# The RWKV state of head 0 copied out of PSUM by ScalarE, that of head 1 by VectorE

## The chip, the cores and the metric

The kernel runs on one core of a Trainium2 chip. The metric is the time of one execution on the device in microseconds (us). The profile comes from one further execution under the hardware profiler; its own time is its span, from the first instruction to the last.

## What is computed

The program is one inference step of a one-layer decoder trunk. A prompt of 1024 tokens with 16 meta tokens ahead of it, and 8 running sequences of 8 new tokens each, go through an input projection, two mixers side by side (RWKV-7 time mixing with 8 heads of 64, and an mLSTM with 4 heads of 128), a gated merge, and an MLP with 4096 hidden columns. What matters here is the RWKV recurrence, which the reference writes token by token:

```
def _rwkv7_step(S, inp):
    r, w, k, v, kk, a = inp
    sa = jnp.einsum('bhvk,bhk->bhv', S, -kk)
    S = S * w[:, :, None, :] + sa[..., None] * (kk * a)[:, :, None, :] + v[..., None] * k[:, :, None, :]
    return S, jnp.einsum('bhvk,bhk->bhv', S, r)
```

Each head has a state S of 64 x 64 that is carried from token to token.

## The kernel before, in words

**Chunks.** The kernel turns the recurrence into chunks of 64 tokens: the work inside a chunk is made into matmuls, and only the state goes from chunk to chunk. The 1152 padded token places make 18 chunks. They are taken in groups of three (`G = 3`), six groups for each of four pairs of heads (`j`), so 24 groups in all. Of the last group of each pair only the first two chunks carry the prompt's state on (its third holds the running sequences), and its second chunk ends in the separate tile `S`, at L889.

**Stages.** Each group passes through four stages, a generator each: `stage_a` (decays and keys, and the strictly triangular matrix X1), `stage_b` (the inverse of a triangular matrix, by forward substitution and three block steps), `stage_c` (the state recurrence and the outputs) and `stage_d` (normalisation of the outputs). The substitution of `stage_b` is a chain of 15 pairs on VectorE, L757 (`tmp`) and L759 (`x`), each of which reads what the one ahead of it wrote. `run_step` runs one step of a software pipeline: stage c of one group beside stage b of the next group and stage a of the one after it, in the hand-written order `ORDER`. Between the pieces, `pull` puts matmuls of the input projection (L277, L279, L281) into TensorE's order as filler.

**The recurrence.** In `stage_c`, for each chunk `c`, two matmuls (one per head, L885) multiply the state tile `Vs` by the transition `GH` into one PSUM tile `pS`: head 0 in partitions 0 to 63, head 1 in partitions 64 to 127. Then two instructions of VectorE (L893, 64 x 65 elements each) scale each half by the decay `lam` and copy it out of PSUM, into the place of `Vs` from which the next chunk's L885 reads. `pS` comes from `cbank()`, a PSUM pool with a single buffer (`c=1`), so the next L885 needs that bank to be read out, too. These copies stand 128 times in the program: 64 chunks of two heads. The output matmuls of a chunk (`ymm`, L841) are issued behind the next chunk's L885.

**What sets the order.** TensorE's order is the program's own order (`manual_schedule` for PE), and so are the fillers' places in it. For VectorE, ScalarE and GpSimd a scheduler at build time decides which instruction stands behind which. It sees an instruction of every stage of the step, and interleaves them. On the chip each engine takes its queue strictly in that order.

Names used below: `wa` (L662, L663 on ScalarE, L669 on VectorE) and `cc` (L672, VectorE) are the decay of stage a; `li`, `lam`, `lx` (L677, L678, L676, ScalarE) come from it; L673, L684, L685, L686, L687 on GpSimd make its keys `KB` and receptances `RB`; L682 and L730 on VectorE are the last of stage a's vector work; L761 and L764 close the substitution.

## Time and profile before

| | us |
|---|---|
| median of 3 runs | 2103.38 |
| lowest, highest | 2100.62, 2105.63 |
| the profiled execution: span | 2102.9 |
| TensorE busy (matmuls) | 1974.6 |
| VectorE busy | 1364.2 |
| ScalarE busy | 704.7 |
| GpSimd busy | 511.1 |

PE is TensorE, PEld its weight loads, DVE is VectorE, ACT is ScalarE, POOL is GpSimd. In a timeline each row gives the start, the duration, the engine, the line and operation, the tiles, and in brackets how long the engine was idle before it and which instruction ended that wait. The RWKV part with its copies lies between about 130 and 850 us of the span.

### The profile page before, as it was taken

Reading aid. Unit: us, or ns where it says so; the run is one execution under the profiler, and the core shown is the slowest. Engines: PE = TensorE matmul, PEld = TensorE weight load, DVE = VectorE, ACT = ScalarE, POOL = GpSimd, SP = SyncE. Lnnn points to the kernel's source line nnn. Section 1 sums busy time; section 2 is a strip of 40 time slices with the busy share of each in tenths; the row PEclk is TensorE's granted clock in tenths of the full one; section 3 lists DMA queues with packets and bytes.
Section 4 is the critical chain, followed back from the end, with each engine's and each line's share of the span. In section 5 each row is a group of like instructions: output and inputs, shape, how many; then the busy total and the mean of one; then the engine's idle time right before and its main releaser. Section 6 shows DMA issues by size and latency. Waiting matters only on the chain.

```text
span 2102.9 us, 32130 instructions
## 1 busy us (share of the span) xinstructions
PE 1974.6 (94%) x12325; PEld 1788.6 (85%) x12325; DVE 1364.2 (65%) x3503; ACT 704.7 (34%) x1654; POOL 511.1 (24%) x392
## 2 busy tenths in 40 slices
PE   8989898999989899989899997999999999999996
PEld 8978788888888788889888886988889999998895
DVE  6478778877887888578776639624444444445447
ACT  7333333333334333254654323331112222222122
POOL 2322122212222222122432404221112212112125
PEclk9999999999999999999999999999999999999998
DMA  5221111212111112231656614211111111111114
GB/s 162 62 68 54 46 52 57 64 45 66 55 51 49 52 61 66 64 107 62 230 175 200 215 60 145 71 51 41 41 41 41 50 51 41 51 41 43 49 32 164
DMA packets 148491, 161.59 MB, mean 77 GB/s; under 512 B 20429, under 2 KB 121607, under 8 KB 148337
## 3 DMA queue, kind: packets, MB, share of 16 engines
q1 hardware_dynamic: 148336, 159.54, 23.7%
q8 instruction: 97, 1.59, 0.3%
q14 instruction: 58, 0.47, 0.1%
HBM read 121.98 MB, written 37.27 MB: 76 GB/s over the span
## 4 chain that ended last, share of the span: by engine, by line
PE 48%; DVE 12%; ACT 2%; DMA 2%; issue 2%; POOL 1%; DVEq 0%; SPq 0%; ACTq 0%; POOLq 0%
PE g L215 11%; PE g L213 11%; PE g L214 11%; PE g L281 2%; PE g L277 2%; PE g L279 2%; PE g L1719 1%; DVE acc L1097 1%; PE g L1619 1%; PE g L1621 1%; PE g L1620 1%; POOL gb L1549 1%; DVE tmp L757 1%; DVE nw L173 1%; DVE ACC L1775 1%
## 5 line engine op out<-in xcount | busy, mean ns | idle before, releaser
L201 POOL TENSOR_TENSOR lo<-raw,hi 128x1024 fp32r<-128x1024 f32 x116 | 280.4, 2422 | 1039.6 <-ACT hi L199 1033.5
L281 PE MATMUL g<-u,lo 128*128 128x414 f32 (+4 forms) x1120 | 388.6, 347 | 1.8 <-POOL lo L201 1.8
L277 PE MATMUL g<-u,hi 128*128 128x414 f32 (+4 forms) x1120 | 387.0, 346 | 2.0 <-ACT gst L527 1.1
L279 PE MATMUL g<-u,hi 128*128 128x414 f32 (+4 forms) x1120 | 386.3, 345 | 0.0
L215 PE MATMUL g<-mg,lo 128*128 128x384 f32 (+1 forms) x768 | 252.3, 328 | 0.0
L213 PE MATMUL g<-mg,hi 128*128 128x384 f32 (+1 forms) x768 | 252.2, 328 | 0.0
L214 PE MATMUL g<-mg,hi 128*128 128x384 f32 (+1 forms) x768 | 252.1, 328 | 0.1
L199 ACT CAST hi<-raw 128x1024 fp32r<-128x1024 f32 x124 | 128.6, 1048 | 342.5 <-PE g L1719 250.9
L1755 DVE TENSOR_TENSOR ACC<-g,ACC 128x512 f32<-128x512 f32 x234 | 159.0, 689 | 111.2 <-PE g L215 105.1
L277 PEld LDWEIGHTS g<-u,hi 128*128 128x128 f32 x1120 | 219.4, 196 | 7.9 <-issue 1.5
L281 PEld LDWEIGHTS g<-u,lo 128*128 128x128 f32 x1120 | 219.6, 196 | 7.4 <-POOL lo L201 2.2
L279 PEld LDWEIGHTS g<-u,hi 128*128 128x128 f32 x1120 | 219.2, 196 | 4.3 <-issue 0.2
L213 PE MATMUL g<-hi,ah 128*128 128x512 f32 (+1 forms) x515 | 202.9, 394 | 0.0
L214 PE MATMUL g<-lo,ah 128*128 128x512 f32 (+1 forms) x515 | 202.7, 394 | 0.0
L215 PE MATMUL g<-hi,ah 128*128 128x512 f32 (+1 forms) x515 | 202.4, 393 | 0.0
L214 PEld LDWEIGHTS g<-mg,hi 128*128 128x128 f32 x768 | 144.6, 188 | 1.1 <-DVE mg L1594 0.4
L213 PEld LDWEIGHTS g<-mg,hi 128*128 128x128 f32 x768 | 144.7, 188 | 0.6
L215 PEld LDWEIGHTS g<-mg,lo 128*128 128x128 f32 x768 | 144.7, 188 | 0.0
L215 PEld LDWEIGHTS g<-hi,ah 128*128 128x128 f32 x515 | 96.7, 188 | 23.0
L213 PEld LDWEIGHTS g<-hi,ah 128*128 128x128 f32 x515 | 96.6, 188 | 22.3
L214 PEld LDWEIGHTS g<-lo,ah 128*128 128x128 f32 x515 | 96.7, 188 | 22.0
L757 DVE TENSOR_TENSOR tmp<-NR,x 128x45 f32<-128x45 f32 (+4 forms) x360 | 97.5, 271 | 20.8 <-DMA NR<-ndr 13.2
(852 smaller groups left out, 3609.3 us busy)
## 6 DMA issues: line engine op xcount, KB each, us to landing
raw<-in_w_in_dram SPq DMA_DIRECT2D x44, 512.0 KB
raw<-in_w_ff_up_dram SPq DMA_DIRECT2D x32, 512.0 KB
raw<-in_w_ff_down_dram SPq DMA_DIRECT2D x32, 512.0 KB
NR<-ndr SPq DMA_DIRECT2D x24, 384.0 KB
gscr<-gst SPq DMA_DIRECT2D x16, 544.0 KB
xt<-in_x_prompt_dram SPq DMA_DIRECT2D x15, 512.0 KB
ga<-gscr SPq DMA_DIRECT2D x8, 544.0 KB
pscr<-ga SPq DMA_DIRECT2D x8, 544.0 KB
```

The costliest lines, as they stand in the source:

```text
L173: V.scalar_tensor_tensor(out=o, in0=a, scalar=c, in1=b, op0=f, op1=g)
L199: nc.scalar.copy(out=hi, in_=raw)
L201: (eng or PO).tensor_tensor(out=lo, in0=raw, in1=hi.bitcast(F32), op=ALU.subtract)
L213: mm(ps, lhsT=wh, rhs=xh, start=(i == 0), stop=False)
L214: mm(ps, lhsT=wh, rhs=xl, start=False, stop=False)
L215: mm(ps, lhsT=wl, rhs=xh, start=False, stop=(i == last))
L277: mm(ps, lhsT=hi[:, k], rhs=xh, start=(k == 0), stop=False)
L279: mm(ps, lhsT=hi[:, k], rhs=xl, start=False, stop=False)
L281: mm(ps, lhsT=lo[:, k], rhs=xh, start=False, stop=(k == 7))
L757: V.tensor_tensor(out=tmp[:, :, :n], in0=NR[:, s + 1:16, :, s].rearrange("p t c -> p c t"), in1=x[:, :, s:s + 1].broadcast_to([128, G, n]) ...
L1097: V.scalar_tensor_tensor(out=acc[:, a:a + m], in0=R[:, a + t_:a + t_ + m], scalar=cw(t_), in1=acc[:, a:a + m], op0=ALU.mult, op1=ALU.add)
L1755: V.tensor_tensor(out=ACC[:, i, cs], in0=ps, in1=ACC[:, i, cs], op=ALU.add)
```

## The change

For each chunk, head 0's copy becomes an activation (function Copy, with the decay as its scale) on ScalarE, and head 1's stays on VectorE:

```
-                    for h, s in enumerate(HP):
-                        V.tensor_scalar(out=Vn[s, cn, h], in0=pS[s], scalar1=lc[s], scalar2=None, op0=ALU.mult)
+                    act(out=Vn[HP[0], cn, 0], in_=pS[HP[0]], func=AF.Copy, scale=lc[HP[0]])
+                    V.tensor_scalar(out=Vn[HP[1], cn, 1], in0=pS[HP[1]], scalar1=lc[HP[1]], scalar2=None, op0=ALU.mult)
```

In the changed kernel L892 is ScalarE's copy of head 0 and L893 VectorE's copy of head 1. The order of TensorE's instructions and of the DMAs is the same in both. On the other three engines the scheduler places instructions anew, around the copies above all. Three places:

**VectorE, the first chunk's copies in the step whose copies run at 357 us.** `x 128x3x9` is a row of the substitution chain with nine columns left; the engines whose signals an instruction waits for stand in brackets. Before:

```order
L759 TENSOR_TENSOR x<-x,tmp 128x3x9 [waits DVE_49]
L893 TENSOR_SCALAR Vs<-c,lam 64x65 [waits PE_49]
L893 TENSOR_SCALAR Vs<-c,lam 64x65
L757 TENSOR_TENSOR tmp<-NR,x 128x3x8 [waits DVE_49]
L669 TENSOR_SCALAR wa<-wa 128x384 [waits Activation_49]
L759 TENSOR_TENSOR x<-x,tmp 128x3x8 [waits DVE_49]
L672 SCALAR_TENSOR_TENSOR cc<-Ct,wa 128x192 [waits DVE_49]
L757 TENSOR_TENSOR tmp<-NR,x 128x3x7 [waits DVE_49]
```

The same place in the changed kernel:

```order
L759 TENSOR_TENSOR x<-x,tmp 128x3x9 [waits DVE_49]
L757 TENSOR_TENSOR tmp<-NR,x 128x3x8 [waits DVE_49]
L759 TENSOR_TENSOR x<-x,tmp 128x3x8 [waits DVE_49]
L757 TENSOR_TENSOR tmp<-NR,x 128x3x7 [waits DVE_49]
L669 TENSOR_SCALAR wa<-wa 128x384 [waits Activation_49]
L893 TENSOR_SCALAR Vs<-c,lam 64x65 [waits Activation_49]
L759 TENSOR_TENSOR x<-x,tmp 128x3x7 [waits DVE_49]
L672 SCALAR_TENSOR_TENSOR cc<-Ct,wa 128x192 [waits DVE_49]
```

Head 0's copy is gone, and head 1's now stands behind four instructions (L757, L759, L757, L669) that stood behind it before. It no longer waits for TensorE but for ScalarE, that is for head 0's copy.

**ScalarE in the same step.** Before:

```order
L663 ACTIVATE wa<-a,PRH 128x192
L677 ACTIVATE li<-cc 128x192 [waits DVE_49]
L678 ACTIVATE lam<-cc 128x192
L676 ACTIVATE lx<-wa 128x192 [waits Pool_49]
L689 COPY bdb<-KB 64x3x64 [waits DVE_49]
```

In the changed kernel:

```order
L663 ACTIVATE wa<-a,PRH 128x192
L892 ACTIVATE Vs<-c,lam 64x65 [waits PE_49]
L677 ACTIVATE li<-cc 128x192 [waits DVE_49]
L678 ACTIVATE lam<-cc 128x192
L676 ACTIVATE lx<-wa 128x192 [waits Pool_49]
L892 ACTIVATE Vs<-c,lam 64x65 [waits PE_49]
L689 COPY bdb<-KB 64x3x64 [waits DVE_49]
```

The first chunk's copy stands right behind L663, the second chunk's right behind `lx`.

**GpSimd, stage a in the step at 217 us** (stage a of the last group of the first pair of heads). Before:

```order
L684 TENSOR_SCALAR wa<-wa,PRM,OKA 128x192
L685 TENSOR_TENSOR wa<-wa,Zk 128x192
L686 TENSOR_TENSOR KB<-wa,li 128x3x64
L687 TENSOR_TENSOR RB_735<-Zr,lam 128x3x64
L854 TENSOR_TENSOR smpD<-Ct,lam 128x256
```

In the changed kernel:

```order
L684 TENSOR_SCALAR wa<-wa,PRM,OKA 128x192
L687 TENSOR_TENSOR RB_735<-Zr,lam 128x3x64
L685 TENSOR_TENSOR wa<-wa,Zk 128x192
L854 TENSOR_TENSOR smpD<-Ct,lam 128x256
L686 TENSOR_TENSOR KB<-wa,li 128x3x64
```

The keys `KB` (L686), for which VectorE's L730 waits, moved behind L687 and L854.

## The prediction

> **What bounds the kernel now.** I read the page's busy times first, then the busy times of the RWKV part alone, then what TensorE waits for there.

> ```profile
> PE 1974.6 (94%) x12325; PEld 1788.6 (85%) x12325; DVE 1364.2 (65%) x3503; ACT 704.7 (34%) x1654; POOL 511.1 (24%) x392
> 120.00:870.00 750.00, 683.31 (x5300) 621.03 (x5300) 594.17 (x2036) 262.05 (x722) 166.33 (x190) 0.95 0.19 56
> ```

> TensorE is the engine that sets the end. In the 750 us around the recurrence it is idle for 750.0 - 683.3 = 66.7 us, VectorE is busy for 79%, ScalarE for 35%. The waits of TensorE in that stretch (us in total, times, the longest):

> ```profile
> PE c L885 <- DVE Vs L893: 47.0, 27, 2.6
> PE a L697 <- POOL KB L686: 5.5, 3, 1.9
> ```

> So 47.0 of the 66.7 us are one wait: the matmul of the next chunk (L885) waits for the copies that the change touches, 27 times. The timeline of one step shows which of its chunks. Its three L885 groups (four rows each, two heads in two passes), with the wait ahead in brackets:

> ```profile
> 353.23 0.39 PE L885 MATMUL c<-Vs,GH 128*64 128x65 f32 x4
> 358.03 0.49 PE L885 MATMUL c<-Vs,GH 128*64 128x65 f32 x4 [2.23 <-DVE Vs L893]
> 362.37 0.34 PE L885 MATMUL c<-Vs,GH 128*64 128x65 f32 x4
> ```

> Only the first chunk's copies are waited for. VectorE in the same step, from just ahead of them, and the second chunk's pair:

> ```profile
> 356.48 0.20 DVE L757 TENSOR_TENSOR tmp<-NR,x 128x30 f32<-128x30 f32 x1
> 356.72 0.19 DVE L759 TENSOR_TENSOR x<-x,tmp 128x30 f32<-128x30 f32 x1
> 356.94 0.20 DVE L757 TENSOR_TENSOR tmp<-NR,x 128x27 f32<-128x27 f32 x1
> 357.17 0.19 DVE L759 TENSOR_TENSOR x<-x,tmp 128x27 f32<-128x27 f32 x1
> 357.39 0.58 DVE L893 TENSOR_SCALAR Vs<-c,lam 64x65 f32<-64x65 f32 x2
> 358.01 0.20 DVE L757 TENSOR_TENSOR tmp<-NR,x 128x24 f32<-128x24 f32 x1
> 358.12 0.35 DVE L669 TENSOR_SCALAR wa<-wa 128x384 f32<-128x384 f32 x1
> 358.38 0.18 DVE L759 TENSOR_TENSOR x<-x,tmp 128x24 f32<-128x24 f32 x1
> ...
> 360.35 0.28 DVE L893 TENSOR_SCALAR Vs<-c,lam 64x65 f32<-64x65 f32 x1
> 360.55 0.16 DVE L759 TENSOR_TENSOR x<-x,tmp 128x18 f32<-128x18 f32 x1
> 360.74 0.29 DVE L893 TENSOR_SCALAR Vs<-c,lam 64x65 f32<-64x65 f32 x1
> ```

> `pS` was ready when the L885 of 353.23 ended, at 353.62, but VectorE came to it at 357.39, since its queue was full. TensorE waits for VectorE's place in its queue, not for the copy's length. The second pair is through at 361.03, and TensorE asks for it at 362.37: 1.3 us to spare.

> **The change part by part.** *Removed from VectorE, added to ScalarE.* 64 copies leave VectorE:

> ```profile
> L893 DVE TENSOR_SCALAR Vs<-c,lam 64x65 f32<-64x65 f32 x128 | 36.4, 285 | 5.9 <-PE c L885 2.9
> L723 ACT COPY Vs<-a 64x65 f32<-64x65 f32 x46 | 9.6, 209 | 0.5
> L938 ACT ACTIVATE sqd<-ys 128x128 f32<-128x128 f32 x4 | 1.2, 312 | 0.1
> ```

> That is 64 x 0.285 = 18.2 us of VectorE. ScalarE's copy with a scale isn't in the trace; a plain one of the same size takes 0.21 us, an activation of twice the width 0.31, and I take 0.25. ScalarE has the time: behind L663 it stands idle for 4.89 us.

> ```profile
> 353.80 0.41 ACT L663 ACTIVATE wa<-a,PRH 128x192 f32<-128x192 f32 x1
> 359.09 0.36 ACT L677 ACTIVATE li<-cc 128x192 f32<-128x192 f32 x1 [4.89 <-DVE cc L672]
> 359.95 0.36 ACT L676 ACTIVATE lx<-wa 128x192 f32<-128x192 f32 x1 [0.24 <-POOL wa L673]
> ```

> So the first copy runs from about 354.2 to 354.5, 3 us before VectorE arrives. The second stands behind `lx`, ends about 360.6, and delays L689 behind it by 0.25 us. Both cost nothing on the path, because VectorE comes to its own half later. By the order, VectorE waits for ScalarE's copy: the two run one after the other, never at once. Where VectorE already waits for TensorE today (2.9 us in that L893 row), 0.25 + 0.29 us in a row takes the place of 2 x 0.285.

> *Moved: the first chunk's copy on VectorE.* This is the term that decides. TensorE needs both halves, since the bank has one buffer. In the step shown, head 1's copy moves behind L757, L759, L757 and L669. Counted from the start of the common row L759 (357.17): today the second copy ends at 357.39 + 0.58 = 357.97, so after 0.80. In the new order three links of the chain come first; links that stand alone follow each other every 0.23 us (356.48 to 357.17 is three links in 0.69). So L757 starts at 0.23, L759 at 0.45, L757 at 0.68. L669 depends on none of them and starts 0.11 after the link ahead of it (358.01 to 358.12), at 0.79. The copy starts only at the end of what stands ahead (357.17 + 0.19 = 357.36, then 357.39), so at 0.79 + 0.35 + 0.03 = 1.17, and ends at 1.46. That is 0.66 us later than today; with the shorter links of other steps I take 0.6. One copy less ahead of it has been counted already.

> [...]

> Ten of the 24 steps have this pattern and nothing that makes up for it: 10 x 0.6 = 6.1. In the first two groups the second chunk's copies have no time to spare either:

> ```profile
> 134.10 0.34 PE L885 MATMUL c<-Vs,GH 128*64 128x65 f32 x4 [2.05 <-DVE Vs L893]
> 160.16 0.34 PE L885 MATMUL c<-Vs,GH 128*64 128x65 f32 x4 [1.94 <-DVE Vs L893]
> 163.21 0.34 PE L885 MATMUL c<-Vs,GH 128*64 128x65 f32 x4 [0.19 <-DVE Vs L893]
> L682 DVE SCALAR_TENSOR_TENSOR bda<-Zk,NKK,lx 64x192 f32<-64x192 f32 x44 | 25.8, 587 | 1.3 <-ACT lx L676 0.6
> ```

> There the order puts an L682 (0.587 us) and one or two more links (0.2 each) ahead of the second copy, and one more VectorE copy is gone: 0.6 + 0.59 + 0.2 - 0.29 = 1.1 us later in the one step and, with the second link, 1.3 in the other, in place of 0.6. Together 2.4. In the other steps of that kind (second chunk, 1.3 us to spare) it is covered, but only just; the cover also grows by the 0.6 us that TensorE comes later.

> In four steps the second wait is long as well, and takes in what the first one gained or lost. In three of them it hangs on GpSimd:

> ```profile
> 222.05 0.34 PE L885 MATMUL c<-Vs,GH 128*64 128x65 f32 x4 [1.99 <-DVE Vs L893]
> 421.45 0.34 PE L885 MATMUL c<-Vs,GH 128*64 128x65 f32 x4 [2.46 <-DVE Vs L893]
> 420.14 0.42 DVE L730 SCALAR_TENSOR_TENSOR wa<-Zr,PRM,wa 128x192 f32<-128x192 f32 x1 [1.06 <-POOL KB L686]
> 218.83 0.59 POOL L686 TENSOR_TENSOR KB<-wa,li 128x192 f32<-128x192 f32 x1
> 219.38 0.72 POOL L687 TENSOR_TENSOR RB<-Zr,lam 128x192 f32<-128x192 f32 x1
> 220.07 0.77 POOL L854 TENSOR_TENSOR smpD<-Ct,lam 128x256 f32<-128x256 f32 x1
> 220.39 0.66 DVE L730 SCALAR_TENSOR_TENSOR wa<-Zr,PRM,wa 128x192 f32<-128x192 f32 x1
> ```

> At 421 us (and 619) L730 waits for `KB`; the copy behind it ends one copy (0.29) earlier, less 0.2 that `cc` comes later: -0.1 each. At 222 `KB` moves behind L687 and L854 and ends 0.72 + 0.77 = 1.5 us later, at about 221.0 with the 0.1 of `cc`; L730 has to start 0.6 later than 220.39, and 0.29 comes off: +0.3. In the fourth (809 us) nothing is left. Of the rest, three steps have only L754 and L669 put ahead: 0.1 each, 0.4. The other five, in which one link is put ahead or nobody waits for the copies, give -0.2 together.

> Sum: 6.1 + 2.4 + 0.3 - 0.2 + 0.4 - 0.2 = 8.8 us. The profiled execution would take 2102.9 + 8.8 = 2111.7; the median is 0.5 above its span, so I forecast **2112 us**, 0.4% slower. From the bounds of the links (half the shift, or everything end to end) and of ScalarE's copy this case has its own range, 2107 to 2117. A measurement of this kernel can tell about 0.2%, 4.2 us, from no change.

> **Why the 18.2 us do not come back.** VectorE is ahead of today by up to 0.86 us when it has done a step's three copies. But it then waits for TensorE in nearly every step, before it comes to the next step's first chunk:

> ```profile
> DVE XC L777 <- PE b L621: 22.3, 21, 2.6
> DVE QZ L787 <- PE b L785: 13.9, 23, 1.5
> DVE sqd L945 <- PE c L614: 7.0, 20, 1.7
> ```

> What it gained is spent there as longer idle time, and from L945 on its queue up to the first copy is the same as before. TensorE's own order is fixed, so a longer wait is not made up for.

> **The rivals.** *VectorE's lead is carried over (faster, 12%).* If those waits aren't real anchors, each step's first copy comes 0.86 us earlier by the relief and 0.6 later by its place: 10 x -0.26, three steps at -0.76, the four double ones together -3.1, the first two together +1.5, the other five -0.5: -7 us, 2096. It decides where VectorE's idle time at L777, L787 and L945 doesn't grow. [...] *The moved instructions fit into gaps (no change, 18%).* If links placed behind L669 or each other cost what they cost between other work (0.11 each in 358.01 to 358.38), the four cost 0.57, less 0.29: 0.28 a step, and the sum is 2.5 us, 2106. The rows of links that stand alone, 0.23 us apart, speak against it. *ScalarE comes late (slower still, 8%).* VectorE now waits for ScalarE with its whole queue behind it, and ScalarE's second copy stands behind `lx`, which waits for GpSimd, or behind an eviction (L527). If it came 0.5 us behind VectorE in some 14 steps of that order and the cover of 1.3 us were used up, it would add 7 us: 2119. Against it stand 360.6 for the copy and 361 or later for VectorE.

> **How the numbers follow.** My case has 62%, the rivals 12, 18 and 8. Slower by over 0.2%: 62 + 8 = 70%; within 0.2%: 18%; faster: 12%. The range leaves out the faster rival and most of the late ScalarE: 2101 to 2118.

> **What would show it.** Right: L885's wait on L893 grows from 47.0 to about 56 us, with 2.8 in place of 2.23 in the step shown; VectorE's copy of the first chunk starts about 0.9 us later behind the same L759, ScalarE's is done long before; VectorE is busy some 18 us less and idles longer at L777, L787 and L945; at 222 us L730 waits for GpSimd. Wrong: the wait per step stays at 2.2 or falls while the order is as shown, or L893 on VectorE is found waiting for ScalarE.

## The result, and the profile after

| | before | after |
|---|---|---|
| median (lowest to highest, runs), us | 2104.51 (2100.62 to 2107.13, 4) | 2122.61 (2120.61 to 2130.45, 4) |
| profiled execution: span | 2102.9 | 2118.8 |
| TensorE busy | 1974.6 | 1984.2 |
| VectorE busy | 1364.2 | 1348.7 |
| ScalarE busy | 704.7 | 718.8 |

The changed kernel takes 1.0093 times as long (95% interval 1.0070 to 1.0115). The sign was forecast, the size was not: 15.9 us more in the profiled executions, where the sum said 8.8, and a median above the range. Below, *place theory* means that TensorE waits for where VectorE's copy stands in its queue; *hand-over rival*, that the two copies' running one behind the other on two engines costs the time; *clock theory*, that a longer wait also slows the matmuls behind it.

The whole difference lies in the recurrence. Its stretch in the profile after (us from and to, its length, then busy time and instructions of PE, PEld, DVE, ACT and POOL, the granted clock, DMA) answers to 120 to 870 us of before:

```profile
120.00:885.00 765.00, 690.75 (x5301) 629.24 (x5301) 581.08 (x1973) 276.03 (x786) 167.69 (x190) 0.94 0.18 55
```

It is 15 us longer, and what follows takes 1233.8 us against 1232.9. TensorE idles for 765.0 - 690.8 = 74.3 us, 7.6 more. But it is also busy for 690.75 - 683.31 = 7.4 us more, with 5301 matmuls in place of 5300. The first half is the forecast. The second half was not in it.

**The waits.** TensorE's and VectorE's, in that stretch of the profile after (us in total, times, the longest):

```profile
PE c L885 <- DVE Vs L893: 57.0, 27, 3.0
```

```profile
DVE X L699 <- PE a L697: 24.7, 19, 3.2
DVE XC L777 <- PE b L621: 24.7, 23, 2.6
...
DVE wa L730 <- POOL KB L686: 11.1, 9, 1.6
...
DVE sqd L945 <- PE c L614: 8.8, 20, 3.5
...
DVE Vs L893 <- ACT Vs L892: 6.4, 10, 1.4
```

L885's wait grew from 47.0 to 57.0 us; about 56 was forecast. TensorE's other idle time shrank by some 2 us. VectorE idles longer, most of all at L699 (12.9 before), less so at L730 (6.7), L777 (22.3) and L945 (7.0), and for 6.4 us it now waits for ScalarE. The step that the prediction showed, TensorE's L885 and then VectorE and ScalarE around the first chunk's copies:

```profile
355.25 0.39 PE L885 MATMUL c<-Vs,GH 128*64 128x65 f32 x4
360.74 0.34 PE L885 MATMUL c<-Vs,GH 128*64 128x65 f32 x4 [2.90 <-DVE Vs L893]
```

```profile
359.25 0.19 DVE L759 TENSOR_TENSOR x<-x,tmp 128x27 f32<-128x27 f32 x1
359.47 0.19 DVE L757 TENSOR_TENSOR tmp<-NR,x 128x24 f32<-128x24 f32 x1
359.69 0.18 DVE L759 TENSOR_TENSOR x<-x,tmp 128x24 f32<-128x24 f32 x1
359.91 0.19 DVE L757 TENSOR_TENSOR tmp<-NR,x 128x21 f32<-128x21 f32 x1
360.02 0.35 DVE L669 TENSOR_SCALAR wa<-wa 128x384 f32<-128x384 f32 x1
360.40 0.29 DVE L893 TENSOR_SCALAR Vs<-c,lam 64x65 f32<-64x65 f32 x1
```

```profile
356.12 0.30 ACT L892 ACTIVATE Vs<-c,lam 64x65 f32<-64x65 f32 x1
```

From the start of the common row L759 (359.25) to the copy's end (360.69) it is 1.44 us; 1.46 was worked out from the order and the old rows. ScalarE's half is done at 356.42, 4 us before VectorE gets to its own. TensorE waits for 2.90 us in place of 2.23.

**The busy time.** TensorE's granted clock fell from 0.971 to 0.966. One wait tells how that comes about. In both kernels L697 waits for GpSimd at the same place of the program, before and after:

```profile
278.87 1.69 PE L697 MATMUL a<-KB,bda 128*128 128x192 f32 x6 [1.84 <-POOL KB L686]
```

```profile
280.90 1.24 PE L697 MATMUL a<-KB,bda 128*128 128x192 f32 x6 [1.85 <-POOL KB L686]
```

TensorE's busy time behind that wait, before and then after (matmuls in brackets, then the granted clock):

```profile
279.50:282.90 3.40, 3.40 (x13) 0.50 0.02 4
282.90:286.30 3.40, 3.40 (x26) 0.99 0.25 75
```

```profile
282.40:285.90 3.50, 3.50 (x26) 1.00 0.04 7
```

Before, the wait was followed by 3.4 us at half clock, in which 13 matmuls ran; after, the clock stayed full, and 26 ran. The clock records of the two traces hold 1.0 and 0.5 alone. The stretches at 0.5 are 3.41, 6.83 or 10.24 us long, but for the last (16.4 us before, 18.2 after), and in each trace all of them start on one grid of 3.41 us. In these two waits what differs is how much of the wait lies in one cell of the grid: before, all 1.84 us; the wait after, at 280.90, straddles two cells, with 0.9 us in one and 1.0 in the other. The first group's wait shows it, too: before (2.05 us, until 134.10) its larger part in one cell is 1.4 us, after (2.68 us, until 135.12) it is 1.9 us:

```profile
132.70:136.10 3.40, 2.00 (x13) 1.00 0.00 0
136.10:139.60 3.50, 3.38 (x28) 1.00 0.00 0
```

```profile
133.20:136.60 3.40, 1.48 (x11) 0.99 0.00 0
136.60:140.00 3.40, 3.40 (x21) 0.50 0.00 0
```

Among the cells that ran at full clock, in this stretch of the two traces, those with 1.9 us of idle time or more were always followed by half clock, those between 1.5 and 1.9 us sometimes, and those with 1.45 or less never, but for three in each trace: they hold no idle time at all, and each holds the 16 matmuls of L904, which are 8 columns wide and take 1.9 us together. What in them brings on the half clock was not tried. Counted in lengths of 3.41 us, the records hold 31 half-clock stretches before and 38 after; with a last one at the program's end, which outlasts the span, it is 122 and 148 us.

### The profile page after: what moved, and what is told of

Same layout as the page of the kernel before. It is cut to its first block, busy times and chain, and to the rows that moved or that the text cites. A ratio compares the mean times of both kernels' runs of the same rounds, so it can differ in the third digit from the quotient of the medians.

```text
span 2118.8 us, 32134 instructions
## 1 busy us (share of the span) xinstructions
PE 1984.2 (94%) x12325; PEld 1798.0 (85%) x12325; DVE 1348.7 (64%) x3439; ACT 718.8 (34%) x1718; POOL 513.4 (24%) x392
## 4 chain that ended last, share of the span: by engine, by line
PE 48%; DVE 12%; DMA 3%; ACT 2%; issue 2%; POOL 1%; DVEq 0%; SPq 0%; ACTq 0%; POOLq 0%
PE g L215 11%; PE g L213 11%; PE g L214 11%; PE g L281 2%; PE g L277 2%; PE g L279 2%; PE g L1719 1%; DVE acc L1097 1%; PE g L1619 1%; PE g L1621 1%; PE g L1620 1%; POOL gb L1549 1%; DVE tmp L757 1%; DMA NR<-ndr 1%; DVE nw L173 1%
## 5 line engine op out<-in xcount | busy, mean ns | idle before, releaser
L277 PEld LDWEIGHTS g<-u,hi 128*128 128x128 f32 x1120 | 222.2, 198 | 8.2 <-issue 1.5
L279 PEld LDWEIGHTS g<-u,hi 128*128 128x128 f32 x1120 | 221.5, 198 | 4.3 <-issue 0.2
L213 PEld LDWEIGHTS g<-hi,ah 128*128 128x128 f32 x515 | 96.6, 187 | 22.3
L757 DVE TENSOR_TENSOR tmp<-NR,x 128x45 f32<-128x45 f32 (+4 forms) x360 | 97.5, 271 | 19.2 <-DMA NR<-ndr 10.9
```

What stands on the lines that cost most here:

```text
L213: mm(ps, lhsT=wh, rhs=xh, start=(i == 0), stop=False)
L277: mm(ps, lhsT=hi[:, k], rhs=xh, start=(k == 0), stop=False)
L279: mm(ps, lhsT=hi[:, k], rhs=xl, start=False, stop=False)
L757: V.tensor_tensor(out=tmp[:, :, :n], in0=NR[:, s + 1:16, :, s].rearrange("p t c -> p c t"), in1=x[:, :, s:s + 1].broadcast_to([128, G, n]) ...
```

## The experiments

**Exchange the engines.** Head 0 stays with VectorE, which goes first; head 1 goes to ScalarE.

```
-                    act(out=Vn[HP[0], cn, 0], in_=pS[HP[0]], func=AF.Copy, scale=lc[HP[0]])
-                    V.tensor_scalar(out=Vn[HP[1], cn, 1], in0=pS[HP[1]], scalar1=lc[HP[1]], ...)
+                    V.tensor_scalar(out=Vn[HP[0], cn, 0], in0=pS[HP[0]], scalar1=lc[HP[0]], ...)
+                    act(out=Vn[HP[1], cn, 1], in_=pS[HP[1]], func=AF.Copy, scale=lc[HP[1]])
```

> Head 0 is copied by VectorE, and then head 1 by ScalarE: the same split, the engines exchanged. By the order VectorE's first copy then stands where the first of the two stood before the change (behind the same row of the substitution chain), and ScalarE's copy waits for it. Place theory: what cost time was the later place in VectorE's queue. TensorE's wait at L885 goes back to 45 to 50 us (57.0 in the changed kernel, 47.0 before), the granted clock to about 0.971, and the time to 2098 to 2107. Hand-over rival: what cost time is that the two copies run one behind the other on two engines, with ScalarE's own queue in between. That is the same here, and the time stays at 2115 to 2123.

Measured: 2101.77 us (median of 12 runs; before 2107.27 in 17), ratio 0.9981 (0.9966 to 0.9996), clock 0.973. TensorE's wait, and ScalarE's:

```profile
PE c L885 <- ACT Vs L893: 44.4, 24, 2.7
```

```profile
ACT Vs L893 <- DVE Vs L892: 92.0, 44, 4.4
```

The split and the hand-over are the same, ScalarE waits for VectorE for 92 us in all, and nothing is lost: VectorE's copy is back at its old place, L885's wait a little below the forecast of 45 to 50 us. The hand-over rival falls.

**Split the first chunk alone; split the others alone.** The condition `c == 0` (then `c > 0`) chooses between the changed pair and the old one.

> Only the first chunk of each group is split between ScalarE and VectorE; the second and third chunk's copies are both VectorE's again. In the order VectorE's first-chunk copy has the late place of the changed kernel. Place theory: the first chunk carries nearly the whole loss, and only the two later copies at 161 and 189 us come back: wait at L885 53 to 57 us, time 2116 to 2122. Rival (ScalarE comes late behind lx for the second and third chunks, 6.4 us of waits of L893 for L892 in the changed kernel): most of the loss goes with them, 2104 to 2112.

> The complement of the run that split the first chunk alone: here the first chunk's copies are both VectorE's, at the place that they had before the change, and only the second and third chunks are split. Place theory: the first chunk's waits are as before, the second chunk's copies are covered except in the first two groups (2.4 us by the sum on record), VectorE's relief is not used: wait at L885 46 to 50 us, time 2102 to 2110 beside a kernel before at about 2107. Rival (the split costs by ScalarE's being late, wherever it stands): 2112 to 2118.

Measured: the first chunk alone gives 2122.05 us, ratio 1.0073 (1.0053 to 1.0093), the others alone 2116.16, ratio 1.0033 (1.0021 to 1.0045). L885's wait in the one and the other:

```profile
PE c L885 <- DVE Vs L896: 55.7, 24, 3.6
```

```profile
PE c L885 <- DVE Vs L896: 55.3, 34, 2.7
```

The first chunk carries most of it; its time lies at the upper end of place theory's 2116 to 2122. The second run lies outside place theory's 2102 to 2110 and inside the rival's 2112 to 2118. Yet a late ScalarE, the rival's cause, does not explain it: VectorE waits for ScalarE for 5.5 us in this run, and for 5.6 us in a run below that takes the old time. What place theory had not seen is seven more waits than before, at the second chunk's copies. The first group:

```profile
139.21 0.34 PE L885 MATMUL c<-Vs,GH 128*64 128x65 f32 x4 [2.05 <-DVE Vs L896]
143.43 0.34 PE L885 MATMUL c<-Vs,GH 128*64 128x65 f32 x4 [1.27 <-DVE Vs L896]
```

```profile
141.74 0.83 DVE L682 SCALAR_TENSOR_TENSOR bda<-Zk,NKK,lx 64x192 f32<-64x192 f32 x1
142.50 0.55 DVE L759 TENSOR_TENSOR x<-x,tmp 128x18 f32<-128x18 f32 x1
143.08 0.29 DVE L896 TENSOR_SCALAR Vs<-c,lam 64x65 f32<-64x65 f32 x1
```

VectorE's copy, behind an L682 and a link, comes too late. Over all groups TensorE waits 17.9 us for the second chunk's copies, in place of 9.0. In the changed kernel it is mostly hidden, since TensorE has already lost its time at the first chunk; so the two losses do not add up.

**Lateness without ScalarE.** The kernel before, the first chunk's pair issued twice:

```
+                    if c == 0:
+                        for h, s in enumerate(HP):
+                            V.tensor_scalar(out=Vn[s, cn, h], in0=pS[s], scalar1=lc[s], ...)
```

> The kernel before, with the first chunk's two copies issued a second time by VectorE (same values to the same place). The place in the queue stays as before, nothing goes to ScalarE; the copies end 2 x 0.29 = 0.57 us later in each of the 24 groups, about what the change did to ten of them and to most others. Place theory: lateness alone is enough. The wait at L885 rises from 47 to 57 to 60 us, the granted clock falls as in the changed kernel (0.971 to about 0.966), and the time is 2117 to 2126, 14 to 22 us more: 0.57 us for some 20 groups, and half as much again by the clock. If a later copy costs its own length only, and the clock has nothing to do with it: 2112 to 2116. Hand-over rival: lateness is not the cause, the time stays below 2112.

Measured: 2129.12 us, ratio 1.0102 (1.0079 to 1.0125), at a clock of 0.966. That is above the 2117 to 2126 of the forecast; the 22 us more than 2107.27 lie at the end of its 14 to 22.

```profile
PE c L885 <- DVE Vs L896: 51.7, 21, 3.3
PE c L885 <- DVE Vs L893: 6.4, 3, 2.2
...
PE b L769 <- DVE XC L761: 4.5, 5, 1.7
```

The waits grew by 58.1 - 47.0 = 11.1 us and by 3 at L769. TensorE's busy time grew by 12 (1986.5 against 1974.6), with the same matmuls. Lateness alone is enough, and costs more than the 14 us of waits that it adds: 22 us by the medians, 25 by the two profiled executions.

**The same operations, the old place.** The changed kernel, with order-only dependencies that keep L669 and the links behind head 1's first-chunk copy (`at` names the link for each group):

```
+                    if c == 0:
+                        cp[:] = ins, at[j > 0][g]
...
+            if cp and s == cp[1]:
+                behind(lk[s], cp[0])
...
+        if cp:
+            behind(w5, cp[0])
```

> The changed kernel, every instruction of it, but with its order in VectorE's queue held near that of before by order-only dependencies: in each group L669 and the links of the substitution chain that the scheduler had put ahead of head 1's first-chunk copy stand behind it again. Place theory: the wait at L885 falls from 57 to 43 to 50 us, and the time from about 2122 to 2098 to 2108, at or a little under the kernel before. Hand-over rival (two engines one behind the other cost it): 2115 or more, with L893's waits for ScalarE as before or longer.

Measured: 2105.70 us, ratio 0.9990 (0.9977 to 1.0003). In this kernel L894 is L885, L901 and L902 are the copies:

```profile
PE c L894 <- DVE Vs L902: 46.4, 27, 3.0
```

```profile
DVE Vs L902 <- ACT Vs L901: 5.6, 9, 0.8
```

VectorE in the same step (L768 and L764 are L759 and L757 here), with the copy back behind the old row:

```profile
352.71 0.19 DVE L768 TENSOR_TENSOR x<-x,tmp 128x27 f32<-128x27 f32 x1
352.93 0.29 DVE L902 TENSOR_SCALAR Vs<-c,lam 64x65 f32<-64x65 f32 x1
```

The same instructions at the old place take the old time, though VectorE still waits 5.6 us for ScalarE. This shows that the loss came from the copy's place in VectorE's queue.

**The clock, first try.** Useless matmuls ahead of the second chunk's L885 in the kernel before:

```
+                if c == 1:
+                    for _ in range(3):
+                        mm(py[:, 256:512], lhsT=ident, rhs=GH.rearrange("p c h k -> p (c h k)")[:, :256], ...)
```

> The kernel before, with three matmuls more in each group, right ahead of the second chunk's L885, where TensorE waits for the first chunk's copies. They write 256 columns of the bank of py that nothing reads. 128 columns of such a matmul take 0.22 us (L814 to L815 in the trace before), so the three take an estimated 1.3 us: 24 x 1.3 = 32 us of useless work for TensorE, most of it inside waits of 2.0 to 2.6 us. The copies stand at the same places. Clock theory: a stretch of 3.41 us in which TensorE idles for more than about 1.8 us is followed by 3.41 us at half clock, which costs 1.3 to 1.5 us. With the wait cut to about 1 us, some 12 of the 20 such stretches go: 12 x 1.5 = 18 us less, against about 5 us more in the five groups whose wait is shorter than the added work: 2085 to 2096, faster than before, and a granted clock of about 0.98. Rival (the clock's dips have nothing to do with these waits): no gain, 2103 to 2112.

Measured: 2165.90 us, ratio 1.0279 (1.0256 to 1.0302), far above both forecasts. This tells nothing of the clock. The scheduler moved the second chunk's copies (L896) behind both L682 and L730, and L885 (now L888) waited there:

```profile
381.35 0.82 DVE L682 SCALAR_TENSOR_TENSOR bda<-Zk,NKK,lx 64x192 f32<-64x192 f32 x1
...
382.30 0.41 DVE L730 SCALAR_TENSOR_TENSOR wa<-Zr,PRM,wa 128x192 f32<-128x192 f32 x1
...
382.82 0.28 DVE L896 TENSOR_SCALAR Vs<-c,lam 64x65 f32<-64x65 f32 x1
```

```profile
383.56 0.34 PE L888 MATMUL c<-Vs,GH 128*64 128x65 f32 x4 [3.17 <-DVE Vs L896]
```

**The clock, with VectorE's order held.** The same matmuls in 12 groups (`g < 3`), and order-only dependencies: both L682, L730 and one link of the chain stay behind the second chunk's copies.

> The useless matmuls once more (three of 256 columns, an estimated 1.3 us, right ahead of the second chunk's L885), on the kernel before, now in the 12 groups alone whose wait there is 1.9 us or more (the first three of each pair of heads), and with VectorE's order held to that of before within one link by order-only dependencies, since in the first try the second chunk's copies moved behind L682 and L730. Clock theory: TensorE idles 0.7 to 1.3 us there in place of 1.9 to 2.6, so some nine stretches of 3.41 us at half clock do not follow; at 1.3 to 1.5 us each that is 12 us less: 2092 to 2100 beside a kernel before at about 2108, with 12 x 1.3 = 16 us more of matmuls in it. Rival (the clock's dips don't hang on these waits): 2106 to 2112.

Measured: 2100.69 us, ratio 0.9962 (0.9948 to 0.9976), clock 0.977. The added group, and what TensorE did in the whole span:

```profile
L894 PE MATMUL s<-GH,Cl 128*128 128x256 f32 x72 | 17.5, 379 | 0.0
```

```profile
PE 1982.9 (94%) x12397; PEld 1793.2 (85%) x12397; DVE 1365.1 (65%) x3503; ACT 704.6 (34%) x1654; POOL 511.8 (24%) x392
```

With 72 useless matmuls, 17.5 us, the kernel is 7 us faster. Without them TensorE is busy for 1982.9 - 17.5 = 1965.4 us, 9 less than in the kernel before, with the same work; the records hold 24 half-clock stretches ahead of the program's end, in place of 31. The held order was not run without the matmuls. But L885's waits for the copies (34.6 us) and the useless work together come to 5 us more than the 47.0 us of waits before, so the gain is not one of earlier copies. It falls some 5 us short of the 12 that were forecast, and the time just misses the range (2092 to 2100), at least in part because the second chunk's L885 now waits as well (0.4 to 0.9 us in most of these groups).

**Take all copies from VectorE; take the first chunk's alone.** Both copies by ScalarE, in all chunks, and then only where `c == 0`.

> Both heads are copied by ScalarE in all three chunks; VectorE copies none (but the tile S). Place theory: TensorE waited for the place in VectorE's queue. ScalarE is idle behind L663, so the first pair is done some 0.5 us after L663, before TensorE asks, and the waits of about 2.2 us at the first chunk go in most groups, about 36 of the 47 us; the second pair stands behind lx on ScalarE and may be 0.5 to 1 us late in some 15 groups. Wait at L885 5 to 20 us. Half-clock stretches behind the first chunk's waits go too, some 12 x 1.3 = 16 us, so the gain is more than the waits alone: 2045 to 2075, and a granted clock of about 0.98. Rival (VectorE's chain is the bound; TensorE would wait for it elsewhere, at L697 or L769): 2085 to 2100, with the same wait moved to those lines.

> Both copies of the first chunk go to ScalarE, those of the second and third chunk stay with VectorE. Place theory: the first chunk's waits go as in the kernel with all copies on ScalarE; the second chunk's copies, which had 1.3 us to spare, are asked for 2.2 us earlier and come 0.57 us earlier, so that some 0.4 us of waiting appear in some 15 groups. Wait at L885 8 to 20 us, 2045 to 2075. Rival (VectorE's chain is the bound): 2085 to 2100.

Measured: 2114.57 us, ratio 1.0021 (1.0006 to 1.0036), and 2108.43, ratio 1.0003 (0.9991 to 1.0016). Both were far off, the place theory's forecasts and the rivals'. A step of the first of the two (its profiled execution, 2104.51 us, is the fastest of twelve):

```profile
351.19 0.39 PE L885 MATMUL c<-Vs,GH 128*64 128x65 f32 x4
...
353.71 0.34 PE L885 MATMUL c<-Vs,GH 128*64 128x65 f32 x4
...
356.90 0.36 ACT L677 ACTIVATE li<-cc 128x192 f32<-128x192 f32 x1 [4.21 <-DVE cc L672]
...
358.42 0.31 ACT L892 ACTIVATE Vs<-c,lam 64x65 f32<-64x65 f32 x1
358.74 0.31 ACT L893 ACTIVATE Vs<-c,lam 64x65 f32<-64x65 f32 x1
...
359.11 0.44 PE L885 MATMUL c<-Vs,GH 128*64 128x65 f32 x4 [2.52 <-ACT Vs L893]
```

The first chunk's wait is gone (353.71 has none). The second chunk's `pS` is there at 354.05, but its copies stand behind `li` and `lx` in ScalarE's queue; `li` waits until 356.90 for VectorE, and TensorE for 2.52 us. Here the wait moved on by one chunk, whole; over the stretch L885 waits 39.2 us for the copies, in place of 47.0. Nor is it VectorE's load: this kernel has 30 us less of it than before (1334.2 busy) and gains nothing. In the second kernel TensorE waits 37.5 us for VectorE's copies, nearly all of it at the second chunk's.

**Then move the place on ScalarE too.** Both copies by ScalarE, `li`, `lam` and `lx` behind the second chunk's pair in the steps whose stage a is of groups 2 to 4, and VectorE's L682 ahead of the last links; then the same for group 5.

```
+        with tc.issue_after(cp[0]) if cp and g in (2, 3, 4) else ExitStack():
...
+            if oc:
+                tc.add_manual_dep(lk[11].ins, ba.ins.name, ...)
...
+        if oc:
+            tc.add_manual_dep(rr.ins, ba.ins.name, ...)
```

> All copies on ScalarE, as in the run before that moved the wait from the first to the second chunk. There the second pair stood behind li, lam and lx, which wait for VectorE's L672, while ScalarE was idle for 4.2 us. Here order-only dependencies put li, lam and lx behind the second pair in the steps whose stage a is of groups 2 to 4, and VectorE's L682 ahead of the last links of the chain. Place theory: the second chunk's waits of 2.3 to 2.7 us go in some 11 groups; TensorE then comes some 1 us early to L697 or L769 and waits there: 11 x 1.3 = 14 us less, and 8 to 10 half-clock stretches less, 10 to 13 us: 2080 to 2098 (2114.6 with the copies on ScalarE but not ordered). Rival (VectorE's chain is the bound, and the wait moves on whole): 2106 to 2116, with 2 us or more per step at L697 or L769.

> The kernel with all copies on ScalarE and the order written out, and the same order-only dependencies also in the steps whose stage a is of group 5 (li, lam and lx behind the second pair of copies, L730's counterpart behind bda), where three waits of 3.2 to 3.4 us were left at the second chunk's L885, with ScalarE idle until li. Place theory: those three waits go, 9.9 us, some 1 us each comes back at the next wait, and two or three half-clock stretches go with them: 8 to 12 us less than the run before, 2083 to 2090 beside a kernel before at about 2108. Rival (the order is no longer what bounds these steps): 2092 to 2100.

Measured: 2096.36 us, ratio 0.9949 (0.9930 to 0.9967), and 2091.12, ratio 0.9925 (0.9909 to 0.9941). Both beat either kernel. The first lies within its forecast. The second lies between its forecast and the rival's, and the intervals of the two overlap, so the last step's own gain is not shown. What is left of TensorE's waits in the first (L893 is L885, L703 is L697, L777 is L769 here):

```profile
PE c L893 <- ACT Vs L901: 13.2, 7, 3.4
PE b L777 <- DVE XC L769: 10.8, 9, 1.2
...
PE a L703 <- DVE bda L686: 9.0, 8, 1.6
```

L885's wait for the copies falls from 39.2 to 13.2 us; 20 us of new waits, each 1.6 us or shorter, take its place at L697 and L769. There TensorE waits for VectorE's chain (XC) and for `bda`. So the rival was in part right: some of the wait came back behind VectorE.

## Why the prediction was half right

**Right: what TensorE waits for.** It waits for the place of the copy in VectorE's queue. In both traces VectorE's instructions around the copies started in the order of that queue: 357.17, 357.39, 358.01, 358.12, 358.38 before, and 359.25 to 360.40 after. With the operations kept and the place restored, the time is that of before (0.9990); with the place kept late and no ScalarE, it is lost (1.0102).

**Right: the term of the first chunk.** Head 1's copy moved behind L757, L759, L757, L669, and the wait grew by 0.67 us in the step shown, 0.66 forecast. L669 again started 0.11 us after the link ahead of it (359.91, 360.02), 0.08 us before that link's end (359.91 + 0.19 = 360.10), so the sum was right to start it there. The range's bound with everything end to end was an estimate that no run shows. All in all the wait at L885 grew by 10.0 us, where the sum had 8.8 (its 10 x 0.6 is 6.0, not 6.1). Errors partly cancel in that: new second-chunk waits of 0.90 us at 192.79 and 0.66 at 457.51, and the steps at 421 and 619 us, which lost 0.3 and 0.2 in place of gaining 0.1 each, against 1.9 in place of 2.4 us in the first two groups.

**Too hopeful: the second chunk's cover.** "Covered, but only just" held in all but two further groups of the changed kernel, but only because the first chunk came late; without that, the cover is used up (the run that split the later chunks alone). ScalarE's copy took 0.306 us (0.25 taken), and VectorE did wait for it, 6.4 us in 10 places, which the prediction had named as a sign of being wrong. The run with the place restored has 5.6 us of that and the old time, so it is not where the time went.

**Right: VectorE's 18.2 us do not come back.** VectorE is busy for 15.5 us less, and the end comes no earlier. But the three rows that were to take up the relief, L777, L787 and L945, grew by only 4.5 us together; L699, which the prediction did not name, grew by 11.8. The faster rival falls with the runs that took more from VectorE and gained nothing until the order was changed as well. (The no-change rival's sum of 2.5 us does not follow from its 0.28 a step: ten such steps alone are 2.8.)

**Wrong: the step from waits to time.** The sum added waits only: "TensorE's own order is fixed, so a longer wait is not made up for", and 2102.9 + 8.8. That took a longer wait to cost its own length, and put the change of TensorE's busy time at nothing. Here it cost more: with 10.0 us more of waits at L885 came 38 half-clock stretches in place of 31. The missing term is TensorE's busy time, 9.6 us over the span (1984.2 - 1974.6) with the same matmuls; with 6.3 us more of idle time it makes the 15.9. It could have been read from the trace of before, around the wait of the step that the prediction shows (358.03):

```profile
354.60:358.00 3.40, 1.20 (x7) 1.00 0.31 93
358.00:361.40 3.40, 3.37 (x16) 0.51 0.00 0
361.40:364.80 3.40, 3.40 (x28) 0.99 0.00 0
```

Half clock stands right behind the wait, and 16 matmuls where 28 fit. Eleven kernels with the same 12325 matmuls give the price (half-clock time from the clock records, 16 to 19 us of it the last stretch at the program's end):

| kernel | half-clock time, us | TensorE busy, us |
|---|---|---|
| all on ScalarE, ordered | 100 | 1966.0 |
| the same, group 5 too | 101 | 1967.1 |
| engines exchanged | 114 | 1971.8 |
| changed, old place | 114 | 1973.1 |
| all copies on ScalarE | 121 | 1972.7 |
| before | 122 | 1974.6 |
| first chunk on ScalarE | 124 | 1975.4 |
| later chunks split | 126 | 1976.7 |
| first pair twice | 147 | 1986.5 |
| changed | 148 | 1984.2 |
| first chunk split | 165 | 1992.0 |

From the first row to the last it is 26.0 us of busy time for 65 us at half clock: 0.40 us each, 1.4 us for a stretch of 3.41. Seven stretches more in the changed kernel are some 9.5 us. How many come up differs from run to run; against the program's first instruction the grid lies anywhere from 0.0 to 3.2 us off in the traces. The 25 runs of the kernel before beside the ordered kernels go from 2100.5 us at a mean clock of 0.974 to 2115.1 at 0.965. So the split of 15.9 holds for these two executions. For the runs there is an estimate from their granted clocks: a mean of 0.970 in the 77 runs of the kernel before, and of 0.965 in the four of the changed kernel, are 127 and 148 us at half clock, and 21 x 0.40 = 8 us of the 18 between the medians.

**Open.** Why the scheduler puts four instructions ahead of a copy that waits for ScalarE, and not of one that waits for TensorE, was not tried; that it takes the copy to be ready later is only argued.

## What to carry to other kernels

An operation that another engine waits for is costed by its place in its queue: if moving half of it makes the other half wait for a second engine, look at what the scheduler puts in between, and fix the order along with the engine, or the wait may just move to the next copy, as it did here (2.52 us at the second chunk's L885, with all copies on ScalarE). Where the trace shows half-clock stretches behind TensorE's waits, a longer wait is costed at more than its growth: here 10 us more at L885 went with 16 to 18 us of time, 14 us more with 22 to 25. There, cutting waits of about 2 us to about 1 us paid 7 us, even with matmuls that nobody reads.
